# A hybrid decoder step on one Trainium2 core: the partitions of sample attention in the order (batch, quarter, token)

## The chip, the cores and the metric

The kernel runs on one core of a Trainium2 chip. The metric is the device time of one execution in microseconds (us). Beside it there is a profile of one execution: a page, and a trace that can be asked for single instructions, waits and stretches of time. Line numbers such as L1106 are lines of the kernel before.

## The reference

One layer of a hybrid decoder is computed for two groups that share the weights: a prompt of 256 tokens, and 8 samples (batch) of 4 new tokens each, which have 1024 past tokens behind them. The change lies in the attention of the samples. Each new token attends, per head (4 heads of 128), to three groups of keys and values with strides 1, 4 and 16, at most 129 keys a group. The three groups are combined under one common maximum:

```python
DEC_BATCH, DEC_SEQ, PAST_LEN = 8, 4, 1024
DIL_GROUPS = ((128, 1), (512, 4), (2048, 16))

def _dilated_group(q, k, v, q_idx, dil, n_back):
    dist = jnp.arange(n_back + 1) * dil
    idx = q_idx[:, None] - dist[None, :]
    ...
    s = jnp.einsum('bqhd,bqjhd->bqhj', q, kg) * (HD_B ** -0.5)
    m = jnp.max(s, axis=-1)
    p = jnp.exp(s - m[..., None])
    return jnp.einsum('bqhj,bqjhd->bqhd', p, vg), m, jnp.sum(p, axis=-1)

# in _dilated_mixture, over the three groups:
    e = jnp.exp(m_all - jnp.max(m_all, axis=0))
    num = sum(e[i][..., None] * parts[i][0] for i in range(N_GROUPS))
    den = sum(e[i] * parts[i][2] for i in range(N_GROUPS))
    return num / den[..., None]
```

Keys and values of the past lie in the caches `cache_win1` (128 rows a sample), `cache_win2` (512) and `cache_win3` (1024). A row of a cache holds a key of 4 x 128 floats (2 KB) and then a value of the same size, so rows are 4 KB apart. The rest of the layer is one wide input projection, a gated delta rule, attention and pooling for the prompt, three gated branch projections (`w_br_a`, `w_br_c`, `w_br_b`), an output projection and a feed-forward part.

## The kernel before

**The weight stream.** All matrices are cut into tiles of 128 x 1024 floats (512 KB). For each tile SP loads `raw` (L169, five buffers), ScalarE casts it to the high half `wh` (L180), VectorE subtracts to get the low half `wl` (L184), and TensorE runs three passes with them (L253 high, L254 with the low half of the input, L255 with the low half of the weights) for all 288 tokens. `wh` and `wl` have three buffers each.

**Work beside it.** Attention, the delta rule and the like are generators. After each tile `step` lets each of them go on by its rate: sample attention (`attn_sample`) 4.4 steps a tile, started when the keys' projection of the last but one group is done; prompt attention (`attn_prompt`) 1. `paced` ties the first of a tile's steps to that tile's `wl`. A scheduler with a model of times lays down each engine's final order. Each engine then runs its instructions in that order, and one that waits holds up all behind it. DMAs of sample attention are issued by POOL (`dq` is `nc.gpsimd`); weights and the pooling history `poolh` (L1229) by SP.

**Sample attention.** The 128 partitions stand for 4 tokens x 8 samples x 4 quarters of the cache; partition p is token x 32 + sample x 4 + quarter. For groups 1 and 2 (strides 4 and 16) a new token t meets only the keys of its own residue, so a tile `kr` of 128 x 512 floats (five buffers, loaded four ahead) holds one key (later one value) for each partition. L1106 loads it from the cache, 32 tiles of group 1 and 16 of group 2 for the keys, and as many for the values. `by_t` (L1086 to L1089) loads the new tokens' own queries, keys and values from the scratch tensor `scr`, one token at a time. For group 0 (stride 1) the partitions are 8 samples x 16 stretches of 8 neighbouring keys, loaded at L1111, and the new ones at L1112. VectorE multiplies each `kr` with the queries (L1142, four heads a tile; sixteen instructions a tile for group 0) and later adds up the values with the weights (L1192).

Between the two, the maxima are exchanged: the partial maxima `mt` (groups 1 and 2) and `m0` (group 0) are written to DRAM (`dmt`, `dm0`), read back as `gm` with one token of one sample in a partition, reduced to `mx`, written as `dmx` and broadcast back into `mt` (L1165) and `m0` (L1167). L1169 and L1171 subtract them from the scores `sct` and `sc0`.

At the end, matmuls with the selector `sel1` (and `sel0` for group 0) sum over the quarters. `maskt` lets the two columns of new tokens count in one quarter only.

**The new tokens' rows.** The projections of queries, keys and values are transposed (`evac_qkv`) into buffers `nat`, and POOL stores them to the outputs (`win_prompt` L986, `win_sample` L991) and to `scr` (L988). The buffers come from a common ring, so a later writer, such as the cast L146, waits until such a store has landed.

Sample attention's loads run from about 392 to 995 us of the span.

Of the kernel before, what the change touches and what calls it, by code (L numbers as in the profile page):

```python
# [9 lines left out]
F32 = mybir.dt.float32  # L10
# [29 lines left out]
def shape_constants():  # L40
    r = np.arange(128)
    t, i = r[:, None], r[None, :]
    same4 = t // 4 == i // 4
    d = {}
    d["ident"] = t == i
    d["U"] = t <= i
    d["V"] = t > i
    d["ones"] = np.ones((128, 128))
    d["Ub"] = (t <= i) & same4
    d["Vb"] = (t > i) & same4  # L50
    d["m32"] = (i // 32 == t // 32 + 1) & ((t // 32) % 2 == 0)
    d["m64"] = (t < 64) & (i >= 64)
    d["mS1"] = same4 & (t % 2 == 0) & (i == t + 1)
    d["mS2"] = same4 & (t % 4 < 2) & (i % 4 >= 2)
    d["blk"] = t // 32 == np.arange(4)[None]
    d["bm"] = (t % 32) // 4 == np.arange(8)[None]
    d["bsel"] = t // 4 == np.arange(32)[None]
    c = np.arange(32)[None]
    d["sel1"] = (t // 32 == c % 4) & ((t % 32) // 4 == c // 4)
    d["sel0"] = np.concatenate([(t // 16 == c // 4) & (c % 4 == tt) for tt in range(4)], axis=1)  # L60
    d["fold"] = t % 32 == i % 32
    d["gsel"] = t % 32 == np.arange(16)[None]
    s0 = t % 16
    m0 = np.zeros((128, 4, 9), bool)
    for tt in range(4):
        m0[:, tt, :8] = s0 * 8 + np.arange(8)[None] >= tt
        m0[:, tt, 8] = ((s0 % 4 == 0) & (s0 // 4 <= tt))[:, 0]
    d["mask0"] = np.where(m0, 0.0, -1e30).reshape(128, 36)
    mt = np.ones((128, 50), bool)
    mt[:, 48:] = t % 4 == 0  # L70
    d["maskt"] = np.where(mt, 0.0, -1e30)
    ic = np.zeros((4, 15))
    for gi, w in enumerate((2, 4, 8, 16)):
        ic[gi] = 1.0 / np.minimum(w, np.arange(15) + 1)
    d["icnt"] = np.broadcast_to(ic.reshape(1, 60), (128, 60))
    for qb, name in ((0, "mp0"), (1, "mp1")):
        parts = []
        for dil in DILS:
            for kb in range(qb + 1):
                dist = (qb * 128 + t) - (kb * 128 + i)  # L80
                ok = (dist >= 0) & (dist % dil == 0) & (dist <= 128 * dil)
                parts.append(np.where(ok, 0.0, -1e30))
        d[name] = np.concatenate(parts, axis=1)
    pack = lambda spec: np.ascontiguousarray(
        np.concatenate([np.asarray(d[n], np.float32) for n, _ in spec], axis=1))
    return pack(C_SPEC), pack(M_SPEC)


class Layer:
# [987 lines left out]
    def attn_sample(self, pool):  # L1077
        nc, c, a, scr = self.nc, self.c, self.a, self.scr
        dq = nc.gpsimd
# [6 lines left out]
        def by_t(dst, kind, g):  # L1086
            src = scr[kind, g].rearrange("(b t) d -> t b d", t=4)
            for t in range(4):
                dq.dma_start(dst[t * 32:t * 32 + 32], src[t][:, None, :].to_broadcast([8, 4, 512]))  # L1089

        for g in (1, 2):
            by_t(qt[:, g - 1], 0, g)
# [3 lines left out]
        cw = [a["cache_win1"][0], a["cache_win2"][0], a["cache_win3"][0]]  # L1096
# [4 lines left out]
        def sources(kv):  # L1101

            for g, dil, n in ((1, 4, 32), (2, 16, 16)):
                src = cw[g].rearrange("b (q m r) k h d -> m k r (b q) (h d)", q=4, r=dil)
                for m in range(n):
                    yield g, (m if g == 1 else 32 + m), lambda kr, s=src[m, kv][:4]: dq.dma_start(kr, s)  # L1106
            for g in (1, 2):
                yield g, 47 + g, lambda kr, g=g: by_t(kr, 1 + kv, g)
            src = cw[0].rearrange("b (s m) k h d -> m k (b s) (h d)", m=8)
            for m in range(8):  # L1110
                yield 0, m, lambda kr, s=src[m, kv]: dq.dma_start(kr, s)  # L1111
            yield 0, 8, lambda kr: dq.dma_start(kr, scr[1 + kv, 0][:, None, :].to_broadcast([32, 4, 512]))  # L1112

        todo = deque((kv,) + r for kv in range(2) for r in sources(kv))
        got = deque()

# [19 lines left out]
        for g, m, kr in rows(0):  # L1136
            for h in range(4):
                hs = slice(h * 128, h * 128 + 128)
                for t in (range(4) if g == 0 else (0,)):
                    q = big[:, t, hs] if g == 0 else qt[:, g - 1, hs]  # L1140
# [7 lines left out]
        mt = pool.tile([128, 4], F32, name="mt")  # L1148
        m0 = pool.tile([128, 16], F32, name="m0")
        nc.vector.tensor_reduce(mt, sct, axis=AX, op=OP.max)  # L1150
        nc.vector.tensor_reduce(m0, sc0.rearrange("p t h m -> p (t h) m"), axis=AX, op=OP.max)
        dmt = self.dr.tile([32, 16], F32, name="dmt")
        dm0 = self.dr.tile([8, 16, 4, 4], F32, name="dm0")
        dmx = self.dr.tile([4, 8, 4], F32, name="dmx")
        dq.dma_start(dmt.rearrange("c (q h) -> (c q) h", h=4), mt)
        dq.dma_start(dm0.rearrange("b s t h -> (b s) (t h)"), m0)
        gm = pool.tile([32, 80], F32, name="gm")
        dq.dma_start(gm[:, 0:16], dmt)
# [2 lines left out]
        yield 4  # L1161
        mx = pool.tile([32, 4], F32, name="mx")
        self.paced(nc.vector.tensor_reduce(mx, gm.rearrange("p (x h) -> p h x", h=4), axis=AX, op=OP.max))
        dq.dma_start(dmx.rearrange("t b h -> (t b) h"), mx)
        dq.dma_start(mt, dmx.rearrange("t b h -> (t b) h")[:, None, :].to_broadcast([32, 4, 4]))  # L1165
        for t in range(4):
            dq.dma_start(m0[:, t * 4:t * 4 + 4], dmx[t][:, None, :].to_broadcast([8, 16, 4]))  # L1167
        yield 4
        self.paced(nc.vector.tensor_tensor(sct, sct, mt[:, :, None].to_broadcast([128, 4, 50]), op=OP.subtract))  # L1169
        s0 = sc0.rearrange("p t h m -> p (t h) m")  # L1170
# [9 lines left out]
        for g, m, kr in rows(1):  # L1180
            for h in range(4):
                hs = slice(h * 128, h * 128 + 128)
                for t in (range(4) if g == 0 else (0,)):
                    dst = o0[:, t, hs] if g == 0 else ot[:, hs]
# [285 lines left out]
def host_layout(x):  # L1470
    f = np.ascontiguousarray
    arr = {n: f(x[n]) for n in PLAIN}
    tok = np.concatenate([x["x_prompt"].reshape(256, 2048), x["x_sample"].reshape(32, 2048)], axis=0)
    arr["xT"] = f(tok.T)
    arr["wba"] = f(x["w_in"][0, :, 4096:4112].reshape(16, 128, 16).transpose(1, 0, 2).reshape(128, 256))
    arr["convh"] = f(x["state_conv"][0].reshape(24, 24, 128).transpose(2, 1, 0).reshape(128, 576))
    arr["poolh"] = f(x["state_pool"][0].reshape(120, 8, 128).transpose(2, 1, 0).reshape(128, 960))
    cols = lambda v: v.reshape(-1, 128).T
    heads = lambda v: np.concatenate(
        [np.concatenate([np.broadcast_to(np.repeat(v[g * 4:g * 4 + 4], 2)[None], (128, 8)),  # L1480
                         np.repeat(v[g * 4:g * 4 + 4], 32)[:, None]], axis=1) for g in range(2)], axis=1)
    sp = {n: cols(x[n][0]) for n in ("g_pre_mix", "g_post_mix", "g_pre_ffn", "g_post_ffn", "pool_scale", "gdn_gain")}
    sp["conv_w"] = x["conv_w"][0].reshape(4, 24, 128).transpose(2, 1, 0).reshape(128, 96)
    sp["dt_bias"] = heads(x["dt_bias"][0])
    sp["a_log"] = heads(x["a_log"][0])
    arr["spack"] = f(np.concatenate([sp[n] for n, _ in P_SPEC], axis=1))
    arr["cpack"], arr["mpack"] = shape_constants()
    return arr
# [32 lines left out]
```

## Time and profile before

| | |
|---|---|
| median of 3 runs | 2064.51 us (2064.17 to 2070.43) |
| the profiled execution | 2068.37 us |
| its span, first to last instruction | 2066.6 us |
| mean granted TensorE clock | 0.992 |
| row loads L1106 | 96, landing after 5.1 / 11.6 / 20.9 us (least, median, most) |
| weight loads L169 of `w_in` | 247, median 4.5 us |

TensorE's busy time is the bound to read first. Its idle time is small, so what another engine does matters only where TensorE waits for it at that moment; the waits and the timeline say where. A DMA's landing time counts from its issue.

### The profile page before, as it was taken

The numbers are of one execution on the slowest core, as the hardware profiler recorded it, in microseconds if no ns is written. First come the engines' busy times: TensorE is split into PE (matmuls) and PEld (weight loads), VectorE is DVE, ScalarE is ACT, GpSimd is POOL, SyncE is SP. The second block draws the span as 40 slices with busy tenths as digits, with TensorE's granted clock in tenths as the row PEclk, the third lists the DMA queues.
The fourth block names the chain that finished last, engine by engine and source line by source line (L and its number), as shares of the span: only waits on it lengthen the run. The fifth ranks groups of instructions, "written<-read, shape, count | busy, mean of one in ns | idle before, by whom it ended". The sixth has DMA issues, their size and how long they took to land. (4 is left out here: it accounts for less than half of the span.)

```text
span 2066.6 us, 38707 instructions
## 1 busy us (share of the span) xinstructions
PE 2010.6 (97%) x15212; PEld 1984.4 (96%) x15212; DVE 1324.2 (64%) x2857; ACT 893.8 (43%) x1414; POOL 291.6 (14%) x504
## 2 busy tenths in 40 slices
PE   8999999999799999989999989999999999999998
PEld 8989998999799999989999989999999999999997
DVE  7969558567688779878875475543554445454555
ACT  6654473453344444333334454334333333333344
POOL 2326312523320022322000000000000000000001
PEclk9999999999999999999999989999999999999999
DMA  8565546959995668998677646766767767677662
GB/s 268 160 182 169 176 140 197 228 173 238 219 205 183 181 184 198 226 220 245 195 229 234 218 160 212 226 222 217 225 216 228 230 217 226 218 225 227 217 205 97
DMA packets 240310, 425.50 MB, mean 206 GB/s; under 512 B 42736, under 2 KB 83200, under 8 KB 238464
## 3 DMA queue, kind: packets, MB, share of 16 engines
q1 hardware_dynamic: 207712, 384.72, 63.1%
q0 software_dynamic: 32272, 37.73, 8.0%
q8 instruction: 119, 1.95, 0.4%
q10 hardware_dynamic: 144, 0.59, 0.1%
q14 instruction: 63, 0.52, 0.1%
HBM read 410.44 MB, written 66.63 MB: 231 GB/s over the span
## 5 line engine op out<-in xcount | busy, mean ns | idle before, releaser
L184 DVE TENSOR_TENSOR wl<-raw,wh 128x1024 fp32r<-128x1024 f32 x585 | 720.2, 1232 | 519.0 <-ACT wh L180 516.7
L180 ACT CAST wh<-raw 128x1024 fp32r<-128x1024 f32 x585 | 612.7, 1050 | 917.9 <-PE m L254 792.3
L253 PE MATMUL m<-hh,wh 128*128 128x288 f32 x1792 | 532.7, 299 | 4.2 <-ACT wh L180 3.7
L255 PE MATMUL m<-hh,wl 128*128 128x288 f32 x1792 | 524.0, 298 | 8.3 <-DVE wl L184 8.3
L254 PE MATMUL m<-hl,wh 128*128 128x288 f32 x1792 | 531.3, 298 | 0.0
L253 PE MATMUL m<-xgh,wh 128*128 128x288 f32 x1408 | 415.8, 297 | 4.0 <-ACT xgh L373 4.0
L254 PE MATMUL m<-xgl,wh 128*128 128x288 f32 x1408 | 415.8, 296 | 3.2 <-DVE xgl L374 3.2
L255 PE MATMUL m<-xgh,wl 128*128 128x288 f32 x1408 | 414.6, 296 | 0.0
L255 PEld LDWEIGHTS m<-hh,wl 128*128 128x128 f32 x1792 | 335.1, 189 | 13.1 <-DVE wl L184 10.7
L253 PEld LDWEIGHTS m<-hh,wh 128*128 128x128 f32 x1792 | 337.7, 189 | 7.8 <-ACT wh L180 4.2
L254 PEld LDWEIGHTS m<-hl,wh 128*128 128x128 f32 x1792 | 338.2, 189 | 1.9 <-issue 1.8
L253 PEld LDWEIGHTS m<-xgh,wh 128*128 128x128 f32 x1408 | 265.5, 189 | 4.6 <-ACT xgh L373 4.3
L254 PEld LDWEIGHTS m<-xgl,wh 128*128 128x128 f32 x1408 | 266.4, 189 | 3.6 <-DVE xgl L374 3.5
L255 PEld LDWEIGHTS m<-xgh,wl 128*128 128x128 f32 x1408 | 265.4, 189 | 0.0
L253 PE MATMUL m<-hidh,wh 128*128 128x288 f32 x704 | 207.5, 295 | 0.0
L254 PE MATMUL m<-hidl,wh 128*128 128x288 f32 x704 | 207.2, 295 | 0.0
L255 PE MATMUL m<-hidh,wl 128*128 128x288 f32 x704 | 206.5, 295 | 0.0
L1449 POOL TENSOR_TENSOR yo<-y,xr 128x288 f32<-128x288 f32 x7 | 5.6, 821 | 1060.7 <-DVE y L1440 1060.7
L254 PEld LDWEIGHTS m<-hidl,wh 128*128 128x128 f32 x704 | 132.4, 188 | 0.0
L253 PEld LDWEIGHTS m<-hidh,wh 128*128 128x128 f32 x704 | 132.2, 188 | 0.0
L255 PEld LDWEIGHTS m<-hidh,wl 128*128 128x128 f32 x704 | 131.9, 188 | 0.0
L1106 POOL DMA_DIRECT2D kr<-cache_win x96 | 65.4, 682 | 250.0 <-DVE junk L1142 136.9
(386 smaller groups left out, 2704.4 us busy)
## 6 DMA issues: line engine op xcount, KB each, us to landing
raw<-w_in SPq DMA_DIRECT2D x247, 512.0 KB, 4.5
raw<-w_gu SPq DMA_DIRECT2D x176, 512.0 KB, 4.0
raw<-w_down SPq DMA_DIRECT2D x88, 512.0 KB, 4.9
win_sample<-cache_win SPq DMA_DIRECT2D x64, 512.0 KB, 5.4
kr<-cache_win POOLq DMA_DIRECT2D x112, 256.0 KB, 10.7
raw<-w_out SPq DMA_DIRECT2D x32, 512.0 KB, 5.0
win_sample<-cache_win SPq DMA_DIRECT2D x32, 508.0 KB, 5.2
st<-state_gdn SPq DMA_DIRECT2D x64, 128.0 KB, 3.2
```

Source lines behind the costliest of these rows:

```text
L180: i = nc.scalar.copy(wh, raw)
L184: self.last_wl = nc.vector.tensor_tensor(wl, raw, wh.bitcast(F32), op=OP.subtract)
L253: nc.tensor.matmul(out, lhsT=wh[:, c], rhs=xh, start=k == 0, stop=False)
L254: nc.tensor.matmul(out, lhsT=wh[:, c], rhs=xl, start=False, stop=False)
L255: nc.tensor.matmul(out, lhsT=wl[:, c], rhs=xh, start=False, stop=k == nk - 1)
L1106: yield g, (m if g == 1 else 32 + m), lambda kr, s=src[m, kv][:4]: dq.dma_start(kr, s)
L1449: (nc.vector if how == "v" else nc.gpsimd).tensor_tensor(out[:, d % 2], y, x, op=OP.add)
```

## The change

Partition p of groups 1 and 2 now stands for sample x 16 + quarter x 4 + token. Four things follow it: the constants (`sel1`, `maskt`), the destinations of `by_t` (every fourth partition instead of 32 neighbours), the source of the row loads (32 x 4 runs of 2 KB, where it was 4 x 32), and the exchange of the maxima, where one broadcast to `mt` becomes four. Group 0 keeps its partitions; `dmx` is laid out by sample and token.

```diff
-    d["sel1"] = (t // 32 == c % 4) & ((t % 32) // 4 == c // 4)
+    d["sel1"] = (t // 16 == c // 4) & (t % 4 == c % 4)
...
-    mt[:, 48:] = t % 4 == 0
+    mt[:, 48:] = (t // 4) % 4 == 0
...
             for t in range(4):
-                dq.dma_start(dst[t * 32:t * 32 + 32], src[t][:, None, :].to_broadcast([8, 4, 512]))
+                dq.dma_start(dst[t:128:4], src[t][:, None, :].to_broadcast([8, 4, 512]))
...
-                src = cw[g].rearrange("b (q m r) k h d -> m k r (b q) (h d)", q=4, r=dil)
+                src = cw[g].rearrange("b (q m r) k h d -> m k (b q) r (h d)", q=4, r=dil)
                 for m in range(n):
-                    yield g, (m if g == 1 else 32 + m), lambda kr, s=src[m, kv][:4]: dq.dma_start(kr, s)
+                    yield g, (m if g == 1 else 32 + m), lambda kr, s=src[m, kv][:, :4]: dq.dma_start(kr, s)
...
-        dmx = self.dr.tile([4, 8, 4], F32, name="dmx")
-        dq.dma_start(dmt.rearrange("c (q h) -> (c q) h", h=4), mt)
+        dmx = self.dr.tile([8, 4, 4], F32, name="dmx")
+        dq.dma_start(dmt.rearrange("(t b) (q h) -> b q t h", t=4, h=4), mt)
...
-        dq.dma_start(dmx.rearrange("t b h -> (t b) h"), mx)
-        dq.dma_start(mt, dmx.rearrange("t b h -> (t b) h")[:, None, :].to_broadcast([32, 4, 4]))
+        dq.dma_start(dmx.rearrange("b t h -> t b h"), mx)
         for t in range(4):
-            dq.dma_start(m0[:, t * 4:t * 4 + 4], dmx[t][:, None, :].to_broadcast([8, 16, 4]))
+            dq.dma_start(mt[t:128:4], dmx[:, t][:, None, :].to_broadcast([8, 4, 4]))
+            dq.dma_start(m0[:, t * 4:t * 4 + 4], dmx[:, t][:, None, :].to_broadcast([8, 16, 4]))
```

The row loads keep their places in POOL's order. On POOL, where the maxima come back (`m` is `m0`), with - for the rows before and + for those now:

```order
-L1164 DMA dmx<-mx 32x4
+L1164 DMA dmx<-mx 4x8x4
 L1237 COPY pst<-xp 128x15
 L1238 COPY pst<-xp 128x120
-L1165 DMA mt<-dmx 128x1x4
-L1167 DMA m_9438<-dmx 128x1x4 x4
+L1166 DMA mt<-dmx 32x1x4
+L1167 DMA m_9438<-dmx 128x1x4
```

The last two rows stand four times in turn, so eight DMAs are issued where five were.

On VectorE, at the same point of the program (`sp` are running sums of the pooling branch, `sc` the scores of group 0), the wait for the maxima is at L1171:

```order
+L184 TENSOR_TENSOR wl<-raw,wh 128x1024 x3
 L1244 TENSOR_TENSOR sp<-xp 128x422
 L1171 TENSOR_TENSOR sc_5912<-sc_5912,m_9438 128x144
-L184 TENSOR_TENSOR wl<-raw,wh 128x1024
 L1244 TENSOR_TENSOR sp<-sp 128x420
-L184 TENSOR_TENSOR wl<-raw,wh 128x1024 x2
+L184 TENSOR_TENSOR wl<-raw,wh 128x1024
```

Three weight tiles' `wl` moved ahead of L1171, which stood in front of them.

On SP, in the stretch of weight loads around the second load of the pooling history `poolh`:

```order
-L169 DMA raw<-w_in 128x2x512 x16
+L169 DMA raw<-w_in 128x2x512 x18
 L1229 DMA poolh<-poolh 128x480
-L169 DMA raw<-w_in 128x2x512 x8
+L169 DMA raw<-w_in 128x2x512 x6
```

That load moved behind two more weight loads. Elsewhere a few matmuls of one bank group change places at `w_br_b`, and one `wl` moves behind a product of the feed-forward part's input.

## The prediction

> **What bounds the kernel now.** I read the page first, then busy time by stretch, then the waits, then the timeline around the longest holes. The page's first part gives the whole span and TensorE's share.
>
> ```profile
> span 2066.6 us, 38707 instructions
> ...
> PE 2010.6 (97%) x15212; PEld 1984.4 (96%) x15212; DVE 1324.2 (64%) x2857; ACT 893.8 (43%) x1414; POOL 291.6 (14%) x504
> ```
>
> TensorE is the bound: it is idle for only 2066.6 - 2010.6 = 56 us. Sample attention runs beside the weight stream on other engines, so this change can only act through those idle us. The view by stretch (busy us per engine with the number of instructions, granted clock, DMA share, GB/s) shows where they lie.
>
> ```profile
> core 0: us, PE busy (x) PEld busy (x) DVE busy (x) ACT busy (x) POOL busy (x), PEclk, DMA share, GB/s
> 500.00:550.00 50.00, 45.90 (x346) 44.86 (x345) 32.15 (x127) 20.33 (x33) 15.43 (x25) 1.00 0.99 220
> 550.00:600.00 50.00, 41.07 (x294) 40.25 (x292) 35.65 (x131) 20.67 (x33) 12.59 (x20) 0.93 0.97 200
> 600.00:650.00 50.00, 50.00 (x383) 49.69 (x382) 42.78 (x158) 22.42 (x34) 10.00 (x18) 1.00 0.82 217
> 750.00:800.00 50.00, 47.35 (x353) 46.66 (x353) 41.85 (x101) 21.60 (x32) 18.88 (x42) 1.00 0.67 182
> 850.00:900.00 50.00, 46.37 (x342) 45.23 (x341) 37.52 (x76) 17.28 (x22) 12.80 (x19) 1.00 1.08 225
> 900.00:950.00 50.00, 44.59 (x323) 44.12 (x322) 39.57 (x78) 16.05 (x19) 16.41 (x26) 0.97 1.06 243
> 570.00:575.00 5.00, 5.00 (x25) 4.97 (x25) 4.83 (x24) 1.48 (x4) 1.09 (x2) 0.60 0.82 173
> 915.00:920.00 5.00, 5.00 (x29) 5.00 (x28) 4.89 (x12) 1.05 (x1) 1.99 (x3) 0.66 1.08 227
> 1300.00:1500.00 200.00, 200.00 (x1512) 200.00 (x1511) 93.24 (x107) 79.09 (x100) 0.00 (x0) 1.00 0.71 223
> ```
>
> Two things stand here. TensorE loses 4.10 + 8.93 = 13.03 us between 500 and 600, and 3.63 + 5.41 = 9.04 between 850 and 950; these are the stretches in which the long rows of groups 1 and 2 (L1106) are loaded. And the DMA engines are not out of capacity: 223 GB/s cost a share of 0.71 after 1300, while 200 to 243 GB/s cost about 1 here. The packets stay longer; there are not more bytes. Next, who waits between 440 and 1070, TensorE's rows and then VectorE's.
>
> ```profile
> PE m L255 <- DVE wl L184: 12.6, 10, 2.8
> PE pv L1065 <- ACT pT L1057: 6.8, 1, 6.8
> ```
>
> ```profile
> DVE ot L1192 <- DMA kr<-cache_win: 21.8, 16, 4.2
> DVE junk L1142 <- DMA kr<-cache_win: 15.0, 8, 4.8
> ...
> DVE sc L1171 <- DMA m<-dmx: 2.2, 1, 2.2
> ```
>
> VectorE stands still 36.8 us for rows of the cache. It works in program order, so the low half of a weight tile (wl, L184) queues behind the waiting row. One such place on the timeline, VectorE and then TensorE:
>
> ```profile
> 912.40 0.35 DVE L1192 SCALAR_TENSOR_TENSOR ot<-kr,sct,ot 128x128 f32<-128x128 f32 x1 [4.16 <-DMA kr<-cache_win]
> 912.67 1.22 DVE L184 TENSOR_TENSOR wl<-raw,wh 128x1024 fp32r<-128x1024 f32 x1
> ```
>
> ```profile
> 913.95 0.40 PE L255 MATMUL m<-och,wl 128*128 128x288 f32 x1 [2.76 <-DVE wl L184]
> ```
>
> 4.16 us of waiting for a row becomes a hole of 2.76. The longest hole of the stage has another road: ScalarE stops at L146, which reuses a buffer that a small store from POOL's queue must first have read (ScalarE, TensorE, and that store's landing, of the one issued at 554.5):
>
> ```profile
> 567.86 0.43 ACT L146 CAST oah<-oa 128x288 fp32r<-128x288 f32 x1 [8.70 <-DMA win_sample<-nat]
> ```
>
> ```profile
> 569.56 0.58 PE L1065 MATMUL pv<-pT,nat 128*128 128x128 f32 x1 [6.82 <-ACT pT L1057]
> ```
>
> ```profile
> DMA to landing us min/median/max: 13.2/13.2/13.2
> ```
>
> The small store takes 13.2 us; it stands in POOL's DMA queue with the row loads, and I put its lateness down to them. So the question is why a row load is slow.
>
> **The change, part by part.** *The row loads (L1106, 96 of them).* Their source was 4 x 32 runs of 2 KB (token outermost); it becomes 32 x 4 (batch and quarter outermost). Bytes, run length, destination and place in POOL's order stay. In the stretch 640 to 760 three forms of the same 256 KB load stand near each other: L1106 with 4 outermost, L1111 with 128, and L1112 with 32 and then 4, which is the form that L1106 gets.
>
> ```profile
> L1106 POOL DMA_DIRECT2D kr<-cache_win x5: 677/679/718, 696.0 to 743.5; - x5
> ...
> DMA to landing us min/median/max: 6.1/6.7/7.5
> ```
>
> ```profile
> DMA to landing us min/median/max: 3.2/3.6/3.8
> ```
>
> ```profile
> L1112 POOL DMA_DIRECT2D kr<-scr x1: 544/544/544, 685.2 to 685.2; - x1
> ...
> DMA to landing us min/median/max: 3.7/3.7/3.7
> ```
>
> With 4 outermost a load takes 6.7 us, with 32 or 128 outermost 3.6 to 3.7, and POOL spends 544 ns on issuing it rather than 679. I read this as a load that is dealt out over few DMA engines in the one form and over all of them in the other. The Trainium skill, "DMA: Bandwidth & Descriptors", section on why a DMA increments its semaphore by 16, states the rule: the number of engines is the largest, up to 16, that divides the outermost counts of both sides. By that rule L1106 runs on 4 engines and would run on 16; its sum would be the one below, and the three landings agree.
>
> Few engines would also explain the rest. Where loads follow each other closely, each waits behind another's long share, and a weight load, spread over all engines, lands with its slowest. Over the whole program the rows of the cache take 10.7 us (median of L1106 and L1111 together) and L1111 alone 4.6, 7.2 at most; weights (L169) take 11.0 between 850 and 950, and 4.0 in the feed-forward stage. Four rows in that order:
>
> ```profile
> kr<-cache_win POOLq DMA_DIRECT2D x112, 256.0 KB, 10.7
> ```
>
> ```profile
> DMA to landing us min/median/max: 3.0/4.6/7.2
> ```
>
> ```profile
> DMA to landing us min/median/max: 7.1/11.0/15.9
> ```
>
> ```profile
> raw<-w_gu SPq DMA_DIRECT2D x176, 512.0 KB, 4.0
> ```
>
> What goes: the idle 13.03 + 9.04 = 22.1 us, and the half clock that followed two of the holes: 5.00 busy us at 0.60 (570 to 575) and at 0.66 (915 to 920) lose 2.0 + 1.7 = 3.7. Together 25.8. What is late next: VectorE is 0.64 to 0.79 busy in those stretches and ran 600 to 650 at 0.86 with TensorE never idle, so it can carry the work. I keep back 5 us: in busy stretches landings will be nearer L1111's 7.2 than its 3.0, the store that ScalarE waits for still shares a queue, and prompt attention starts its work at 550 to 560 on the same VectorE. I take 20.8, between 0 (loads as late as now) and 25.8 + 2.65 (the idle time of 750 to 800 goes as well).
>
> *Strided destinations for tokens and queries (L1089).* Twenty-four loads of 32 partitions, as many and as large as before, to every fourth partition instead of 32 neighbours; no row shows that form. The nearest pair, L1106 and L1112, differs by 3.0 us in landing, and rows are loaded four ahead of their use: I take 0, and 3 us either way as bounds for the keys and for the values.
>
> *The exchange of the maxima (L1155 to L1167).* The maximum for the window groups comes back in four DMAs instead of one, each ahead of one of the four of group 0: eight issues instead of five. POOL's rows now, the second showing what it does behind them, and VectorE's first use of that:
>
> ```profile
> 760.50 2.41 POOL L1167 DMA_DIRECT2D m<-dmx  x4
> ...
> 766.71 1.55 POOL L1236 COPY xp<-poolh 128x120 f32<-128x120 f32 x2 [1.80 <-DMA poolh<-poolh]
> ```
>
> ```profile
> 782.11 0.68 DVE L1244 TENSOR_TENSOR sp<-xp 128x422 f32<-128x422 f32 x1
> ```
>
> At 2.41 / 4 = 0.60 each, three more issues delay the last landing by 1.8 us, and VectorE already waits 2.2 there. But three wl now stand ahead of that wait (the rows above), so weights are no longer queued behind it: of the 2.65 us that TensorE loses in 750 to 800, between 1.8 more and 1.7 less; I take 0. SP's load of the pooling history moves behind two weight loads, some 6.3 us later at 3.17 us a tile (below); POOL's copies of it end at 768.3 now and VectorE first reads them at 782.1. Without that cover, one wl behind it would cost up to those 6.3 us once.
>
> *Masks and selectors* are the same tiles with other numbers: 0. *Reordering at w_br_b and at the start of the feed-forward* swaps equal instructions within a bank group; I take 0, bounds one wl (1.22 us) either way each.
>
> **The sum.** The profiled execution took 2068.37 us, 1.8 of it outside its span: 2068.4 - 20.8 = 2047.6. The median of the runs shown is 2064.5, 3.9 below that execution; the three runs spread over 6.3 us, and late loads are the kind of thing that varies. From the median the same sum gives 2043.7. I forecast 2046.
>
> **Rivals.**
> *Half of it:* the loads gain less than their form promises. A row's four tokens become neighbours, but the 32 groups still lie 512 KB or 1 MB apart, and now several engines start on such addresses at the same moment. If landings fall only halfway, to some 8 us, half the sum goes: 2064.5 - 10.4 = 2054 to 2058. L1111 and L1112, with 32 KB and 2 KB between their runs, can't rule this out. The Trainium skill, same page, section "Latency and other measured facts", reports that copies at row pitches that are large powers of two fall from 207 to 103 GB/s, and suspects colliding streams; no run here shows it. Chance 0.11.
>
> *It does not do what it says:* the loads land late because the stage is simply full of traffic, or the order of dimensions is not what counts. Then nothing moves: 2064. Against it stand 223 GB/s at a share of 0.71, and L1112. Chance 0.08.
>
> *Slower:* rows spread over all engines stand in front of every weight load on every engine, where now only some are held up. A landing of 11.0 becomes later instead of earlier. The point from which it decides is 15.9 us, five raw buffers at the 3.17 us that TensorE takes for a tile (1512 matmuls in 200 us, 24 to a tile): the present maximum of 15.9 just touches it. Each of some 60 tiles in the two stretches then late by 0.2 us costs 12: 2076. Against it: 600 to 650 has L1111's wide loads and no hole. Chance 0.05.
>
> **How the numbers follow.** Forecast 0.76, half 0.11, nothing 0.08, slower 0.05. The low end is the whole 28.5 off the median, 2036; the high end is the half-way rival's, 2058; that leaves out nothing, slower and a little of the forecast. A measurement of this kernel tells about 0.3% (6.2 us) from no change. Faster by more: 0.76 and most of the half-way case, 0.85; within: 0.11; slower: 0.04.
>
> **What would show it.** L1106 landing at 4 to 6 us and issued in about 545 ns; VectorE's 36.8 us for cache rows below 8; ScalarE's waits for win_sample below 5 us; weights landing at 4 to 6 us between 500 and 950; TensorE's 500 to 600 and 850 to 950 at 48 us or more of each 50, without a stretch of lower clock; DMA share near 0.75. The forecast is wrong if L1106 still lands after 9 us, or if it lands early and TensorE waits as long for wl or wh because of something else: VectorE's own load, or ScalarE at L146.

## The result, and the profile after

The changed kernel takes 2040.54 us (median of 4 runs, 2037.63 to 2041.33), the kernel before 2064.34 beside it (4 runs, 2059.7 to 2070.43): a ratio of 0.988, with a 95% interval of 0.9853 to 0.9908, or 23.8 us less. The forecast was 2046, the range 2036 to 2058. The profiled execution took 2040.06 us, its span 2038.3, against 2068.37 and 2066.6: 28.3 us less in both. Timed a second time, the same kernel took 2040.72 (2038.74 to 2041.72).

The page's row of busy engines, POOL's DMA queue (packets, MB, share of 16 engines), and the row loads (count, size, median landing in us):

```profile
PE 2001.1 (98%) x15212; PEld 1978.0 (97%) x15212; DVE 1328.0 (65%) x2857; ACT 894.4 (44%) x1414; POOL 271.9 (13%) x507
q0 software_dynamic: 13936, 37.58, 5.6%
kr<-cache_win POOLq DMA_DIRECT2D x112, 256.0 KB, 3.9
```

The loads land after 3.9 us at the median, not 10.7. The queue's row of the page before, for comparison:

```profile
q0 software_dynamic: 32272, 37.73, 8.0%
```

The bytes are the same, but 18,336 packets are gone: 191 for each of the 96 loads. The change left the count and length of the rows alone, so this is a different way of dealing a load out, and it can be read on the page without opening the trace. L1106's landings over the whole program and then in the quiet stretch 640 to 760 (where before had 6.1/6.7/7.5), and the weight loads' landings in 850 to 950 (before 7.1/11.0/15.9), in three answers:

```profile
DMA to landing us min/median/max: 2.8/3.9/9.1
```

```profile
DMA to landing us min/median/max: 3.0/3.5/3.7
```

```profile
DMA to landing us min/median/max: 3.5/4.6/6.9
```

The stretches that held the idle time (columns as in the prediction):

```profile
500.00:550.00 50.00, 50.00 (x384) 49.90 (x384) 41.93 (x155) 23.87 (x38) 17.33 (x32) 1.00 0.85 261
550.00:600.00 50.00, 50.00 (x380) 49.69 (x379) 42.22 (x161) 23.72 (x37) 9.75 (x19) 1.00 0.70 217
750.00:800.00 50.00, 48.79 (x364) 47.99 (x362) 47.43 (x110) 26.56 (x40) 12.82 (x26) 1.00 0.76 241
850.00:900.00 50.00, 50.00 (x380) 50.00 (x379) 45.88 (x88) 17.66 (x20) 13.85 (x23) 1.00 0.78 242
900.00:950.00 50.00, 50.00 (x382) 50.00 (x381) 45.63 (x96) 18.91 (x23) 11.81 (x20) 1.00 0.76 235
```

TensorE is never idle between 500 and 600 or between 850 and 950, at full clock, and 261 GB/s now cost a DMA share of 0.85 where 220 cost 0.99. The waits from 440 to 1070, TensorE's largest and then VectorE's largest for a DMA:

```profile
PE m L253 <- ACT obh L146: 0.8, 1, 0.8
PE m L255 <- DVE wl L184: 0.7, 1, 0.7
```

```profile
DVE mx L1163 <- DMA gm<-dm: 0.9, 1, 0.9
```

VectorE's 36.8 us for rows of the cache are gone. ScalarE's two largest waits for a DMA before were these:

```profile
ACT oah L146 <- DMA win_sample<-nat: 17.9, 2, 9.2
ACT wh L180 <- DMA raw<-w_in: 17.7, 7, 3.3
```

They are gone too; one of 2.1 us for another DMA is all that it still waits for one (in the second profile of this kernel 1.4 us for the store and 2.1 for another DMA).

**Where the 28.3 us came from.** The windows' idle time of TensorE from 500 to 1000 fell from 25.2 us to 1.2, so by 24.0. In the first 500 it rose by 0.6. TensorE's busy time fell by 9.5 (2010.6 to 2001.1). 5.1 of that is half clock: in the stretches that the trace marks with a granted clock of 0.5 TensorE is busy for 19.0 us in the program before and for 8.9 now, each us costing half of one. Of the 19.0, 7.9 stood behind the two holes that the prediction names; 3.4 near 1066 come and go, since the second profile of the changed kernel has such a stretch near 1033. Of the other 4.4, 3.9 are the first matmuls behind 15 holes: in the trace each adds 0.39 us of busy time there and 0.13 at the same place now. So such a hole costs about a quarter of a us beyond its idle time, as the profile counts it (it models where matmuls end). That makes 32.9, more than the 28.3 that the span lost.

**What was given back at the end.** The last store of the output lands 2032.4 us into the span, against 2065.4 before. From there to the end of the span, before and then after:

```profile
2065.40:2066.60 1.20, 0.00 (x0) 0.00 (x0) 0.00 (x0) 0.00 (x0) 0.00 (x0) 0.50 0.00 0
```

```profile
2032.50:2038.30 5.80, 0.00 (x0) 0.00 (x0) 0.00 (x0) 0.00 (x0) 0.00 (x0) 0.50 0.00 0
```

Nothing computes and no byte moves, for 1.2 us before and 5.8 after. The trace's instruction records, which the views leave out here, show what is waited for: the closing DRAIN of POOL. It begins 4.3 us before the last landing in both, and takes 4.0 us before, hidden behind the stores, and 9.3 now. So the change earned 32.9 us in the profiled pair and paid 4.6 of them at the end.

### The profile page after: what moved, and what is told of

Read it like the earlier page. It is cut to its first block, busy times and chain, and to the rows that moved or that the text cites. A ratio compares the mean times of both kernels' runs of the same rounds, so it can differ in the third digit from the quotient of the medians.

```text
span 2038.3 us, 38713 instructions
## 1 busy us (share of the span) xinstructions
PE 2001.1 (98%) x15212; PEld 1978.0 (97%) x15212; DVE 1328.0 (65%) x2857; ACT 894.4 (44%) x1414; POOL 271.9 (13%) x507
## 3 DMA queue, kind: packets, MB, share of 16 engines
q0 software_dynamic: 13936, 37.58, 5.6%
## 5 line engine op out<-in xcount | busy, mean ns | idle before, releaser
L1449 POOL TENSOR_TENSOR yo<-y,xr 128x288 f32<-128x288 f32 x7 | 5.6, 820 | 1059.5 <-DVE y L1440 1059.5
L1106 POOL DMA_DIRECT2D kr<-cache_win x96 | 52.1, 543 | 248.7 <-DVE junk L1142 145.5
```

What stands on the lines that cost most here:

```text
L1449: (nc.vector if how == "v" else nc.gpsimd).tensor_tensor(out[:, d % 2], y, x, op=OP.add)
```

## The experiments

My theory: a load with 4 outermost runs goes over few DMA engines and one with 32 over all, and everything else follows from the landing time. The rivals: neighbouring runs are what counts (a token's four rows now follow each other in the cache); the stores behind ScalarE's waits, not the rows, are the cause; or the loads are only issued too late. Ratios are to the kernel before, run beside each kernel.

| kernel | built on | median us (runs) | ratio, 95% interval |
|---|---|---|---|
| one_dma_a_token | before | 2106.77 (4) | 1.021 (1.0195 to 1.0225) |
| groups_25_7 | after | 2052.61 (1) | one run, no interval |
| groups_31_1 | after | 2261.78 (1) | one run, no interval |
| groups_16_16 | after | 2037.76 (4), again 2038.48 (4) | 0.9869 (0.9855 to 0.9884), 0.9881 (0.9866 to 0.9896) |
| stores_by_sp | before | 2064.96 (10) | 1.0008 (0.9998 to 1.0018) |
| own_buffers | before | 2056.82 (10) | 0.9967 (0.9946 to 0.9988) |
| one_more_ahead | before | 2066.96 (10) | 1.0007 (0.9993 to 1.0021) |
| two_fewer_ahead_old | before | 2105.27 (4) | 1.0201 (1.0181 to 1.0222) |
| two_fewer_ahead | after | 2040.22 (4) | 0.9889 (0.9875 to 0.9904) |
| exchange_twice | after | 2041.14 (4) | 0.9885 (0.9868 to 0.9901) |
| after_again | after | 2040.72 (4) | 0.9892 (0.9875 to 0.9908) |

### Wide loads in the old order of partitions

The kernel before, with each row load as four DMAs, one for each token:

```diff
-lambda kr, s=src[m, kv][:4]: dq.dma_start(kr, s)
+lambda kr, s=src[m, kv][:4]: [dq.dma_start(kr[t * 32:t * 32 + 32], s[t]) for t in range(4)]
```

> The kernel before, with its partition order, masks and exchange; only each row load of groups 1 and 2 is issued as four DMAs, one for each token: 32 partitions from 32 runs that lie 512 KB or 1 MB apart. Theory A (what counts is over how many DMA engines a load is dealt out): 32 outermost gives wide loads, each lands after 3 to 5 us, VectorE's waits for cache rows fall below 8 us of now 36.8, and the time comes to 2038 to 2048, although POOL issues four times as many DMAs (about 2.2 us for a tile instead of 0.68). Theory B (what counts is that a token's run now has its three neighbours beside it in memory): no runs are neighbours here, so the loads stay slow and the time stays at 2060 to 2068. Theory C (masks, exchange or the scheduler's other order did it): 2060 to 2068 as well, but with loads that land early.

The added line moves those behind it by one, so L1106 is L1107 here and L1192 is L1193; the next three kernels have the same shift. The loads, two stretches, and TensorE's longest wait between 1070 and 1200:

```profile
kr<-cache_win POOLq DMA_DIRECT2D x384, 64.0 KB, 3.6
```

```profile
900.00:950.00 50.00, 50.00 (x381) 50.00 (x380) 35.90 (x63) 18.56 (x21) 23.41 (x46) 1.00 0.76 223
1050.00:1100.00 50.00, 7.15 (x43) 3.83 (x42) 42.33 (x117) 3.04 (x6) 1.61 (x3) 0.55 0.25 90
```

```profile
PE so L1201 <- DVE big L1193: 42.0, 1, 42.0
```

No time that was expected came. The loads land early, VectorE waits for none, and 900 to 950 is whole, all with the old order of partitions and no neighbouring runs. But with 384 issues the scheduler laid the program out otherwise: sample attention ends late, and TensorE stands for 42 us at its end. The kernel speaks for the theory in its landings, and its time says nothing of the change.

### Only the number of engines

The changed kernel, its load cut into two DMAs by groups of four rows: 25 and 7, then 31 and 1, then 16 and 16. Bytes, rows, neighbours and number of DMAs are the same in the three, and VectorE's and TensorE's orders too.

```diff
-lambda kr, s=src[m, kv][:, :4]: dq.dma_start(kr, s)
+lambda kr, s=src[m, kv][:, :4]: [
+    dq.dma_start(kr[x * 4:y * 4], s[x:y]) for x, y in ((0, 25), (25, 32))]
```

> The changed kernel; each row load is issued as two DMAs, of 25 groups (100 partitions) and of 7 groups (28 partitions), the four neighbouring tokens still innermost. Theory A, with the rule that the number of engines is the largest up to 16 that divides the outermost counts: 5 engines and 7, so the larger DMA puts 20 runs on an engine where 8 are now and 32 were before; between 3.5 us (now) and 6.7 (before) for loads in the quiet stretch that is about 5.1, and the time lands between the two kernels, 2042 to 2056. If the odd count is dealt out over all 16 after all: as the changed kernel, 2036 to 2044. Theory B: as the changed kernel, 2036 to 2044.

> The changed kernel; two DMAs for each row load, of 31 groups (124 partitions) and of 1. Same order of VectorE and TensorE as with 25 and 7. Theory A with the rule of the largest common divisor up to 16: 31 is prime, so one engine carries all 124 runs, 62 packets where it has 4 now: a load lands after 12 us or more even in the quiet stretch, after 20 and more in the busy ones, more than the four loads ahead cover, and the kernel becomes clearly slower than before: over 2090. If an odd count is dealt out over all engines, or if neighbouring tokens are what counts: 2036 to 2046.

> The changed kernel; each row load is issued as two DMAs of 16 groups (64 partitions) each. VectorE's and TensorE's order is the same as with 25 and 7 groups, so the two differ in how the loads are dealt out alone. Theory A (number of engines): both halves go over 16 engines, loads land after 3 to 5 us, and the time is that of the changed kernel, 2036 to 2046. If the 2052.6 us of 25 and 7 groups came from issuing two DMAs for a tile, this one is at 2048 to 2056 as well.

Landings of both halves in the quiet stretch 640 to 760, for 25 and 7, for 31 and 1, and for 16 and 16:

```profile
DMA to landing us min/median/max: 3.7/4.4/5.2
```

```profile
DMA to landing us min/median/max: 15.6/17.7/20.1
```

```profile
DMA to landing us min/median/max: 2.4/2.7/3.4
```

With 25 and 7 the packets are 27760 and VectorE and ScalarE wait again:

```profile
DVE ot L1193 <- DMA kr<-cache_win: 9.0, 7, 2.6
DVE junk L1143 <- DMA kr<-cache_win: 5.3, 5, 2.6
```

```profile
ACT oah L146 <- DMA win_sample<-nat: 12.5, 2, 6.7
```

With 31 and 1 VectorE's first wait and the queue's row are

```profile
DVE junk L1143 <- DMA kr<-cache_win: 112.3, 13, 14.8
```

```profile
q0 software_dynamic: 106096, 38.31, 8.0%
```

All three times lie where the theory put them. Cut at 16 the load is as fast as whole; cut at 31 the kernel loses 220 us. How the 32 groups are divided decides, so it is not the bytes, the neighbours or the second issue, nor the size of the piece, since the whole load lands in 3.5. Worked out by the rule of the Trainium skill, "DMA: Bandwidth & Descriptors", section on why a DMA increments its semaphore by 16, 31 outermost runs go to one engine, 25 and 7 to 5 and 7, and 16 to all 16; the order of the landings (17.7, 4.4, 2.7) agrees.

The traces show the number itself. For each load they hold sixteen signals on the semaphore that counts its landing, which I take as one from each DMA engine. In one load of each kernel they come so, in us after its issue:

| load | early signals | last signals |
|---|---|---|
| before, at 708.0 | 12, at 2.0 to 2.6 | 4, at 6.3 to 6.7 |
| after, at 691.2 | none apart | 16, at 2.6 to 3.6 |
| 25 of 25 and 7, at 714.5 | 11, at 1.7 to 1.8 | 5, at 3.7 to 4.5 |
| 31 of 31 and 1, at 652.8 | 15, at 3.9 to 4.3 | 1, at 17.8 |
| 16 of 16 and 16, at 679.8 | none apart | 16, at 2.0 to 2.5 |

The engines that still work when the others have signalled number 4, 16, 5, 1 and 16, as the theory has it. Other loads of this stretch that stand alone divide in the same way.

### ScalarE's road

The longest hole before (6.82 us) came through ScalarE, which waited for a small store. Two kernels on the one before: the stores issued by SP instead of POOL, and the stores' `nat` in buffers of their own, so that no cast waits for them.

```diff
-self.dq.dma_start(o[:, WIN[g] - 4:, kind - 1, cs], n[:NS, :256])
+nc.sync.dma_start(o[:, WIN[g] - 4:, kind - 1, cs], n[:NS, :256])
```

```diff
-n = self.U(name="nat")
+n = self.U(name="nat") if tb < 2 else self.small(256, "nats", 3)
```

> The kernel before, with its slow row loads; the stores of the new tokens' rows (L986, L988, L991) are issued by SP instead of POOL, so that they no longer stand in one DMA queue with the row loads. If ScalarE's road (it waits at L146 for such a store) is as I read it, the two holes it makes, 2.75 us near 533 and 6.8 near 569 with 2.0 of half clock behind it, go, and VectorE's holes stay: 2050 to 2056. If those stores were late for another reason (the DMA engines themselves), ScalarE waits as long as before and the time stays at 2060 to 2068.

> The kernel before, narrow loads and all; the new tokens' rows are kept in three buffers of their own before they are stored, so that the cast at L146 no longer reuses a buffer that such a store must first have read. If ScalarE's waits at L146 make the holes near 533 and 569 (2.75 and 6.8 us and 2.0 of half clock), these go and the time falls to 2050 to 2057. If the holes only come later, because weights and rows are late anyway: 2058 to 2066, with ScalarE's waits at L146 gone and more waits for raw.

In SP's queue the stores are as late: ScalarE waits 16.6 us for them, where it was 17.9. Its waits in the first kernel:

```profile
ACT oah L146 <- DMA scr<-nat: 8.3, 1, 8.3
ACT oah L146 <- DMA win_sample<-nat: 8.3, 1, 8.3
```

It is not the queue that they stand in; with rows on 4 engines a store is late from either. With buffers of their own ScalarE no longer waits for them, and the median falls by some 7 us (0.9967; by the interval 2.5 to 11), at the upper edge of what was expected. So this road holds about a third of the 23.8, and by the interval anything from a tenth to a half. The profile of that kernel is of its slowest execution (2073.24), so its holes are not read.

### More or fewer loads in flight

`KR` sets the buffers of `kr`; 6 means five loads ahead, 3 means two.

```diff
-KR = 5
+KR = 6
```

> The kernel before with six buffers for the row loads instead of five, so five are loaded ahead instead of four; the loads stay narrow. Theory A: a load keeps landing after 10 us and more, but has one more tile's time (about 3 us) before it is needed: VectorE's 36.8 us for cache rows fall to about a third, ScalarE's road and late weights stay, and the time comes to 2050 to 2058. If VectorE's waits don't make TensorE's holes, the time stays at 2060 to 2068 with waits that fall.

> The kernel before with three kr buffers instead of five (KR = 3). Theory that narrow loads are late because of their own engines: with 6.7 us for a load that stands alone, two ahead cover some 6 us and no longer one whole landing, so VectorE waits more for rows than the 36.8 us of before, 60 us or more, and the time is 2075 us or more. Rival, that fewer loads in flight land sooner and stop holding up weights and stores (a sixth buffer brought nothing): landings fall below 8 us, ScalarE's waits for stores shrink, and the time stays at 2055 to 2068 us.

> The changed kernel with three kr buffers instead of five (KR = 3), so a row load is issued two ahead of its use instead of four. Theory that the landing time is what counts: loads land in 3.9 us at the median and 9.1 at most, and a row is used about every 3 us, so two ahead covers some 6 us: nearly all loads are still in time and the time stays within 2036 to 2048 us, with some 5 us of VectorE waits for rows. Rival, that the depth of five buffers is what carries the gain: VectorE waits more than 25 us for rows, TensorE's 500 to 600 shows holes again, and the time goes to 2055 us or more.

VectorE's waits for rows before with 6 buffers, before with 3, and after with 3:

```profile
DVE ot L1192 <- DMA kr<-cache_win: 19.3, 12, 3.8
DVE junk L1142 <- DMA kr<-cache_win: 5.8, 2, 5.6
```

```profile
DVE junk L1142 <- DMA kr<-cache_win: 55.5, 28, 6.5
DVE ot L1192 <- DMA kr<-cache_win: 41.4, 22, 5.4
```

```profile
DVE ot L1192 <- DMA kr<-cache_win: 5.8, 6, 1.9
```

Before, a deeper queue of loads takes 11.7 us off VectorE's waits, while ScalarE's grow (for `win_sample` from 17.9 to 22.8, for `raw` of `w_in` from 17.7 to 31.7), and the median stays: issuing the loads earlier does not help, and my 2050 to 2058 was wrong. This profile, too, is of the kernel's slowest execution (2073.34), so how much of ScalarE's growth is due to the sixth buffer is not shown. With 3 buffers the loads land earlier (8.1 us median instead of 11.6) and ScalarE waits 7.5 us for the stores instead of 17.9, as the rival there said; but two ahead don't cover 8.1 us, and the time follows the rows, as the theory said: 2105. After, the same cut costs nothing: 2040.22. So the gain hangs on the landing time and not on the depth, and two of the five buffers could now be given up.

### The exchange, and the two halves again

The eight DMAs that bring the maxima back, issued twice:

```diff
-for t in range(4):
+for t in range(8):
+    t %= 4
```

> The changed kernel; the eight DMAs that bring the maxima back are issued twice, so POOL issues 16 where the changed kernel has 8 and the one before 5: about 4.8 us more on POOL. As I put the three added DMAs at 0, because weights no longer stand behind the wait: within 2 us of the changed kernel, 2038 to 2044. If the exchange is on the path: 3 to 5 us more, 2043 to 2046.

VectorE's only wait for them:

```profile
DVE sct L1170 <- DMA mt<-dmx: 0.3, 1, 0.3
```

The time is 0.6 us above the changed kernel's. Its closing idle stretch is 0.6 us longer too (6.5 us instead of 5.8 from the last landing to the last instruction), so doubling the exchange cost nothing where it stands.

> The changed kernel with each row load issued as two DMAs of 16 groups, once more, beside the changed kernel itself on the same chip. The first time it took 2037.8 us where the changed kernel's runs have a median of 2040.5. If halved loads are worth something (4.3 us landings of smaller DMAs leave gaps for weights), it is 2 to 3 us faster than the changed kernel here too, with its interval below that one's. If it was chance, the two medians lie within 1.5 us.

> The changed kernel unaltered, for the comparison with the load in two halves on the same chip: 2038 to 2042 us, 0.988 of before.

2038.48 (2036.27 to 2039.81) against 2040.72: the expected 2 to 3 us, but the ranges overlap, so the halved load is at best 0.1% better. The profiles say that the loads are not the reason. The last store lands at 2031.8 and 2032.8 us in its two profiles and at 2032.4 and 2032.9 in the changed kernel's; what follows is shorter:

```profile
2031.80:2035.90 4.10, 0.00 (x0) 0.00 (x0) 0.00 (x0) 0.00 (x0) 0.00 (x0) 0.50 0.00 0
```

## Why the prediction was right, point by point

*The row loads.* Landing of 4 to 6 us and 545 ns of issue were to be seen; it is 3.9, and 543. The mechanism is shown from both sides: an odd cut brings the late loads back, an even one does not, and the signals of single loads give the number of engines.

*The rivals.* "Half of it" asked for landings of some 8 us from addresses 512 KB or 1 MB apart; in the quiet stretch they are 3.5, and L1111's, with 32 KB, 3.4. The Trainium skill ("DMA: Bandwidth & Descriptors", "Latency and other measured facts") has 207 GB/s at a row pitch of 512 KB and 164 and 103 only from 2 MB up, for larger copies from other queues; 1 MB is not in its list, so it gave the rival less support than the prediction reads into it, and these loads don't contradict it. "It does not do what it says" falls with the cut at 31. "Slower" asked for weights landing later than 11.0; they land after 4.6.

*The sum.* This is where the forecast was off: 20.8 us in the sum, 28.3 in the profiled pair. The step that failed is the 5 us kept back for landings in busy stretches, for the store and for prompt attention's work on VectorE: all 22.1 us of idle time in the two stretches went, and 1.9 more from 750 to 850. The term for half clock was 3.7 and came to 5.1, of which 3.9 behind the two holes that it was worked out from. The other 4.4 us of busy time, nearly all of it first matmuls behind holes, were in no term. Against these stands a cost that was in none either, the 4.6 us of the closing drain. 2047.6 from the profiled execution was 7.5 too high; 2043.7 from the median was 3.2 too high, since the execution that was profiled before lay 4 us above the median. That 2046 came so near is in part luck: the drain took back about as much as the first matmuls gave.

*ScalarE at L146.* That the rows are behind the store's 13.2 us was right (such stores now land after 3.8 at the median, 5.9 at most), that POOL's queue is the way was not: SP's queue is no better.

*The exchange and the reordering.* Taken at 0, between 1.8 more and 1.7 less, and the lower bound came. Of the 1.9 us from 750 to 850, 1.7 was one hole, in which TensorE waited for the `wl` behind L1171, where VectorE waited 2.2 us for the maxima:

```profile
767.58 0.40 PE L255 MATMUL m<-hh,wl 128*128 128x288 f32 x1 [1.67 <-DVE wl L184]
```

Both waits are gone; whether by the new order of `wl` or because the maxima now come in time, no run separates. The three added DMAs cost nothing that the doubled exchange could show. *Strided destinations* were taken at 0: the new tokens' keys and values (`kr<-scr`) land after 4.0 us at the median, where it was 8.0, and VectorE doesn't wait for them. POOL waits 3.9 us for the load of `poolh` (1.8 before), and VectorE shows no wait behind it.

## What to carry to other kernels

Before ordering partitions, write down the outermost counts of each load's two sides: 4 or 31 there can make the same 256 KB land two to five times later than 32, and the lateness spreads to loads and stores that only share the engines. A queue's packet count on the page, out of proportion to its bytes, gives it away, and more prefetch doesn't cure it. Look also behind the last landing, where a gain can be given back unseen.

## What the runs showed of the hardware that was not expected

POOL's closing DRAIN has a length of its own for each kernel, from the instruction records. It begins 4.3 us (4.6 in one) before the last landing everywhere:

| kernel | DMAs on POOL | packets of its queue | drain, us | last landing to last instruction, us |
|---|---|---|---|---|
| before | 221 | 32272 | 4.0 | 1.2 |
| one_dma_a_token | 509 | 18448 | 3.7 | 1.2 |
| stores_by_sp | 171 | 30352 | 3.7 | 1.1 |
| groups_31_1 | 320 | 106096 | 3.0 | 1.5 |
| groups_25_7 | 320 | 27760 | 5.7 | 2.5 |
| groups_16_16 | 320 | 15472 | 7.3 | 4.1 |
| after, and two_fewer_ahead | 224 | 13936 | 9.3 | 5.8 |
| exchange_twice | 232 | 14192 | 10.0 | 6.5 |

Two profiles of the same kernel agree within 0.01 us (after and after_again; groups_16_16 twice), and `KR` moved it by 0.1 at most, so it belongs to the DMAs that a kernel issues on POOL, not to chance or time. Neither their number nor their packets orders the table, and what it does wait for stays open. That POOL could begin its drain earlier, without its last additions of the output (L1449), and hide all of it, was not tried.
